# Who makes the low part of a weight tile: VectorE by a subtraction, or ScalarE and an accumulating DMA

## The chip, the cores and the metric

The kernel runs on one NeuronCore of a Trainium2 chip. The metric is the device time of one execution in microseconds, from launch to end; lower is better. Engines are called as in the profile: PE is TensorE's matrix multiplications, PEld its weight loads, DVE is VectorE, ACT is ScalarE, POOL is GpSimd, SP is SyncE. SP and POOL start most of the transfers here; the transfers themselves run on 16 DMA engines.

## The reference, cut to what matters

Two layers of a transformer work on 128 prompt tokens and 512 sample tokens of width 1024. Each layer has three token mixers side by side (a retention, a differential attention and a latent attention, called MLA), merged through sigmoid gates, and then a gated feed-forward net (FFN) of inner width 2816. All is float32. What matters is that nearly everything is a product of activations and weights:

```python
def _layer(x, mod, lw, lam_init, rope, ctx):
    sh1, sc1, g1, sh2, sc2, g2 = jnp.split(mod, 6, axis=-1)
    h = _rmsnorm(x, lw['norm1_g']) * (1.0 + sc1) + sh1
    mix, ctx_out = _mixers(h, lw, lam_init, rope, ctx)
    x = x + g1 * mix
    h = _rmsnorm(x, lw['norm2_g']) * (1.0 + sc2) + sh2
    x = x + g2 * _swiglu(h, lw['w_ffn_in'], lw['w_ffn_out'])
    return x, ctx_out

def _swiglu(h, w_in, w_out):
    a, b = jnp.split(h @ w_in, 2, axis=-1)
    return (jax.nn.silu(a) * b) @ w_out
```

## The kernel before, in words

A product in float32 is made of three products in a shorter format, float32r. Each operand is split into a high part, which is the value rounded to float32r, and a low part, which is what the rounding left out; then hi·hi + hi·lo + lo·hi is summed in one PSUM bank. Where the weights are the stationary operand, these are lines 131 to 133 (`mm3`) and 1087 to 1089 (`mm_outer`, which walks the contraction in the outer loop and several outputs in the inner one).

All weights pass through `load_w`, in 298 units. A unit is a tile of 128 rows and at most 1024 columns of float32, up to 512 KB: `raw` comes from DRAM by a transfer that SP starts (L120), ACT copies it into `whi` (L112, called from L123), and DVE subtracts `whi` from `raw` into `wlo` (L115, called from L124). The three kinds of tile rotate through buffers of their own: 3 for `raw`, 4 for `whi`, 4 for `wlo`. A buffer is used again when its last reader is done. So the copy of unit n waits until PE has gone through unit n - 4, and the transfer of unit n until the subtraction of unit n - 3 is done.

The work of a layer runs in this order. The latent attention (`mla`) has small weight units of its own (`w_qp`, `w_qk`, `w_v`), and between its steps `fill()` puts pieces of the differential attention's projections (`diff_proj`, six pairs of units), whose results go to DRAM by transfers that POOL starts (L773). Then come the first branch product, the differential attention with gates and retention values between its steps (stores by POOL, L790), the retention with the second merge, and the third merge (`branch`). `out_proj` and `ffn` follow. The FFN goes through 22 inner columns in three parts of 8, 8 and 6: for each column two `w_ffn_in` units (L1089 is the line that reads their low parts), and after each part eight `w_ffn_out` units (L1146). The FFN's opening makes its first two columns in halves, so that it needs four units at once and then the next two.

From the third merge of layer 0 on, `ada_rows` loads 80 blocks of modulation weights (`rawr`, 512 KB each, 3 buffers) by transfers that POOL starts (L235), and DVE reduces each in two instructions (L238).

The order of the instructions on each engine isn't the order of the program text: the framework plans it with a simulated timeline of its own and then writes one fixed list for each engine. Engines run their lists in order and wait on semaphores.

Of the kernel before, what the change touches and what calls it, by code (L numbers as in the profile page):

```python
# [12 lines left out]
F32 = mybir.dt.float32  # L13
# [8 lines left out]
P = 128  # L22
# [3 lines left out]
T = 640  # L26
# [9 lines left out]
NA = 416            # columns of the first product of the latent attention; 256 more follow  # L36
FFN_PARTS = ((0, 8), (8, 16), (16, 22))

# columns of the constant table
C_ID, C_ONE, C_DF, C_DB, C_SEL, C_VEC = 0, 128, 256, 384, 512, 514  # L40
C_C64, C_S64, C_C32, C_S32, C_END = 520, 776, 1032, 1160, 1288
# columns of the per-partition parameter table
V_ADA, V_N1, V_N2, V_FG, V_QN, V_KVN, V_END = 0, 96, 112, 128, 136, 142, 146
# columns of the replicated-row table
# [3 lines left out]
class Kern:  # L48
# [25 lines left out]
    def G(self):  # L74
        """A bank for a product: two in turn, one of them only while attention has the other."""
        self.gi ^= 1
        tag = "G" if self.gi or self.filling else "O"
        return self.ps.tile([P, 512], F32, tag=tag, name="G", bufs=1)
# [11 lines left out]
    def plan(self, points, *gens):  # L90
        """Spread the pieces of (generator, number of pieces[, from, to]) evenly over the next calls of fill()."""
        order = []
        for j, (_, n, *span) in enumerate(gens):
            t0, t1 = span or (0.0, 1.0)
            order += [(t0 + (t1 - t0) * (i + 0.5) / n, j) for i in range(n)]
        self.queue = [(t * points, gens[j][0]) for t, j in sorted(order)]
        self.point = 0
# [19 lines left out]
    def load_w(self, src, cols):  # L117
        """A weight unit [128, cols] from DRAM, as a part that float32r holds and the rest."""
        raw = self.w.tile([P, cols], F32, tag="raw", name="raw", bufs=3)
        self.nc.sync.dma_start(out=raw, in_=src)  # L120
        hi = self.w.tile([P, cols], F32R, tag="whi", name="whi")
        lo = self.w.tile([P, cols], F32R, tag="wlo", name="wlo")
        self.split_hi(hi, raw)  # L123
        self.split_lo(lo, raw, hi)  # L124
        return hi, lo

    def mm3(self, out, steps):
        """out = sum of lhsT^T rhs over steps of (lhs_hi, lhs_lo, rhs_hi, rhs_lo)."""
        n = len(steps)
        for i, (lh, ll, rh, rl) in enumerate(steps):  # L130
            self.pe.matmul(out, lh, rh, start=i == 0, stop=False)  # L131
            self.pe.matmul(out, lh, rl, start=False, stop=False)  # L132
            self.pe.matmul(out, ll, rh, start=False, stop=i == n - 1)  # L133

    def rsqrt(self, out, ssq, n, mul, mul2=1.0):
        """out = mul2 / sqrt(ssq * mul + EPS), for [128, n]."""
        v = self.sm.tile([P, n], F32, tag="rs_v", name="rs_v")
        a = self.sm.tile([P, n], F32, tag="rs_a", name="rs_a")
        y = self.sm.tile([P, n], F32, tag="rs_y", name="rs_y")
        self.dve.tensor_scalar(v, ssq, mul, EPS, op0=ALU.mult, op1=ALU.add)  # L140
        self.dve.tensor_scalar(y.bitcast(I32), v.bitcast(I32), 1, None, op0=ALU.arith_shift_right)
        self.dve.tensor_scalar(y.bitcast(I32), y.bitcast(I32), -1, 0x5F3759DF, op0=ALU.mult, op1=ALU.add)
        for it in range(4):
            self.dve.tensor_tensor(a, y, y, op=ALU.mult)
            self.dve.scalar_tensor_tensor(a, a, -0.5, v, op0=ALU.mult, op1=ALU.mult)
            self.dve.scalar_tensor_tensor(out if it == 3 else y, a, 1.5, y, op0=ALU.add, op1=ALU.mult)
        if mul2 != 1.0:
            self.dve.tensor_scalar(out, out, mul2, None, op0=ALU.mult)
# [7 lines left out]
    def setup(self):  # L156
# [12 lines left out]
        # silu of the two conditioning vectors, padded to 32 columns  # L169
# [7 lines left out]
    def rows_setup(self):  # L177
        # log_sigmoid(x) = min(x, 0) - log1p(exp(-|x|)), log1p(e) = 2 atanh(e / (2 + e))
# [38 lines left out]
    def ada_vectors(self, pool):  # L217
        """silu of the two conditioning vectors on every partition."""
        d = self.dve
        cs = self.csr = self.load_small(pool, [P, 2, 1024], self.io["condr"], "csr")  # L220
        for i in range(2):
            th = pool.tile([P, 1024], F32, tag="rawr", name="csth", bufs=3)
            self.act.activation(th, cs[:, i, :], AF.Tanh, scale=0.5)
            d.scalar_tensor_tensor(th, th, 1.0, cs[:, i, :], op0=ALU.add, op1=ALU.mult)
            d.tensor_scalar(cs[:, i, :], th, 0.5, None, op0=ALU.mult)

    def ada_rows(self, l, b0, b1, pool):
        """Modulation with output columns on partitions and the sums on VectorE, a column block a step."""
# [16 lines left out]
    def mod_scale(self, l, which):  # L245
        """A = norm_g * (1 + sc) as [128, 8, 2]; which 0 for the mixers, 1 for the ffn."""
# [10 lines left out]
    def square(self, h, k, x, pool):  # L257
        """Adds the squares of row tile k of a half of x to its sum."""
# [26 lines left out]
    def modulate(self, l, which, h, k, xn, a, ht, pool):  # L285
        """Row tile k of h = xn * A + sh, in float32r parts."""
# [13 lines left out]
    def norm(self, l, which, h, x, a, pool, ps):  # L300
        """h-th half of rmsnorm(x) * A + sh from the sum of squares, in float32r parts (hi, lo) [128, 8, n]."""
# [9 lines left out]
    def start(self):  # L311
        """First norm and first part of the first product, as the columns of the modulation come in."""
# [79 lines left out]
    def tok(self, act, k, b):  # L392
        """(hi, lo) stationary block b of an activation in two halves."""
# [4 lines left out]
    def a_steps(self, act, b, units):  # L398
        """For 128 tokens of block b, act^T W; units: list of (hi, lo, first k, n k) with [128, nk, N]."""
# [17 lines left out]
    def rope(self, pool, out, x, b, nb, nh, hd, tag="avs"):  # L417
        """out = rope(x) for sample blocks b .. b + nb: x [128, nb, nh, hd]."""
# [13 lines left out]
    def softmax(self, sv, p, z, scale, tot=None):  # L432
        """p = exp(scale (sv - max sv)), tot = sum p, z = 1 / tot, for one score row a partition in sv."""
# [7 lines left out]
    def mla(self, l, act, yraw, pool, first=None):  # L441
# [10 lines left out]
        # the k tiles hold two heads each time: rows 0:64 k_nope, rows 64:96 k_pe  # L452
        NK = 3
        kts = [pool.tile([P, 2, TK], F32R, name=f"kt{i}") for i in range(NK)]
        for g in range(2):
# [12 lines left out]
            if g == 0:  # L468
                self.rsqrt(rs[:, 0, :], ss[:, 0, :], NB, 1.0 / 256)
                # decoupled keys  # L470
# [15 lines left out]
                # compressed keys and values  # L486
# [43 lines left out]
        # decoupled queries of all heads, by tokens  # L530
# [81 lines left out]
    def mla_av(self, pool, v, hh, blks, pt, n, y, last=None):  # L612
        """y [64, n] += p^T v over key blocks; pt(kb) gives (hi, lo) [128, n]."""
# [11 lines left out]
    def mla_head(self, pool, qt, q0, kt, v, hh, y, last=None):  # L625
        """Two blocks of sample queries of one head."""
# [55 lines left out]
    def diff(self, l, act, yhi, ylo, ctx):  # L682
# [4 lines left out]
        # lambda  # L687
# [12 lines left out]
        def build(hd):  # L700
# [8 lines left out]
            # keys  # L709
# [24 lines left out]
            # queries, as hi(q1) lo(q1) lo(q2) hi(q2)  # L734
# [24 lines left out]
    def diff_proj(self, l, act, pool):  # L759
        """Queries, keys, values of the differential attention, by tokens, to DRAM; a generator."""  # L760
# [15 lines left out]
    def ret_values(self, l, act, pool):  # L776
        """Values and doubled silu gates of the retention, by tokens, to DRAM; a generator."""
# [15 lines left out]
    def diff_head(self, pool, Q, K1, K2, V, nlam, lam_init, yhi, ylo):  # L793
# [3 lines left out]
        for b in (1, 2, 3, 4, 0):  # L797
# [19 lines left out]
            # p0 / t0 - lam p1 / t1 = (p0 - (lam t0 / t1) p1) / t0, the last division after the product with v  # L817
# [39 lines left out]
    def ret(self, l, act, yraw, ctx):  # L857
# [6 lines left out]
        # decay matrices by (key, query), with the key scale  # L864
# [13 lines left out]
        # projections  # L878
        qkT = pool.tile([P, 2, 2, T], F32, name="qkT")       # (q, k), head pair: rows are 2 heads x 64
        QX = pool.tile([P, 4, T - 128], F32, name="QX")      # per head: rows xi_f q | xi_b q  # L880
        V = pool.tile([P, NB, 512], F32, name="rV")
        SG = pool.tile([P, NB, 512], F32, name="rSG")
        S0 = pool.tile([P, 4, 4, 128], F32, name="rS")       # block, head: states before the block (f | b)
# [5 lines left out]
        for which in (1, 0):  # L889
            units = self.load_a(io["w_ret"][l, which], 2, 4, 256)  # L890
            for b in range(NB):
# [23 lines left out]
                # sums over the chunk: forward states at once, backward ones once all are there  # L915
# [15 lines left out]
        for b in range(NB):  # L931
            self.fill()
            sc = self.S()                        # even heads in one bank, odd ones in the other
# [40 lines left out]
    def branch_first(self, l, g, yhi, ylo, m):  # L974
        """m = y W of the first branch; its gates come later."""
# [10 lines left out]
    def gates(self, l, g, act, m, pool):  # L986
        """m *= 2 sigmoid(gate logits); a generator."""
# [11 lines left out]
    def branch(self, l, g, act, yhi, ylo, m, pool, last):  # L999
        """m += 2 sigmoid(gate logits) * (y W); a generator."""  # L1000
# [50 lines left out]
    def tail(self, unit, load, n0, a, b, mid):  # L1051
        """Units (n, half) for n0 <= n < 8, half a's first; mid once half a is done."""
# [28 lines left out]
    def mm_outer(self, outs, steps, hook=None):  # L1081
        """Products of which each one's row tile k comes before row tile k + 1 of any; hook after a few."""
# [10 lines left out]
    def ffn(self, l, act, x, pool, xp, hook, a, b, mid):  # L1093
# [21 lines left out]
        # the first two columns by halves, the second half's norm within the first half's products  # L1115
# [159 lines left out]
def consts():  # L1275
# [5 lines left out]
    dist = i[None, :] - i[:, None]                # query minus key, at (key, query)  # L1281
# [23 lines left out]
def ntiles(w):  # L1305
    """[K, N] -> [N / 128, 128, K / 128 * 128]: column tiles, rows on partitions."""
# [4 lines left out]
def pieces(w, nk):  # L1311
    """[K, N] -> [K / 128 / nk, 128, nk N]."""
# [4 lines left out]
def layout(inputs):  # L1317
# [17 lines left out]
    st = np.concatenate([g["state_ret_fwd"][0], g["state_ret_bwd"][0]], axis=2)     # l, h, 128, 128  # L1335
# [59 lines left out]
```

## Time and profile before

| | |
|---|---|
| time, median of 2 runs | 2521.03 us (2520.76 to 2521.29) |
| the profiled execution's own time, first to last instruction | 2522.9 us |
| PE busy | 2471.6 us (98%) |
| DVE busy | 1500.7 us (59%) |
| ACT busy | 987.9 us (39%) |
| POOL busy | 170.8 us (7%) |
| mean granted TensorE clock | 0.995 |
| SP's queue of weight transfers | 164.12 MB, 19.6% of 16 engines' span |
| POOL's queue of transfers | 81.36 MB, 9.8% |

The profile is of one execution on the chip. Its span, from the first to the last instruction, is 2522.9 us, which is 1.9 us over the median of the timed runs; there is no other measure of that execution, so sums made against the profile are made against this span. "Busy" counts an engine's own instructions. A wait is put down to the instruction whose semaphore came last. The chain is followed back from the last instruction through what released each step.

### The profile page before, as it was taken

To read this page: it belongs to the slowest core of one execution; us is meant where nothing else is said; L and a number is where in the kernel's file an instruction comes from. 1 tells how busy PE (TensorE), PEld (TensorE's weight loads), DVE (VectorE), ACT (ScalarE), POOL (GpSimd) and SP (SyncE) were. 2 spreads that over 40 slices of the span, in tenths; PEclk is the share of its full clock that TensorE was granted. 3 is DMA by queue.
4 is the path that set the end of the run, shared out by engine and by line. 5 is a ranking of instruction groups with operands and counts; after the bars stand their busy time and mean duration, and the time that the engine had idled before them with its cause. 6 is when DMAs were issued, how large, how long until landed. Compare 5 with 4: busy or idle time off the path is not lost.

```text
span 2522.9 us, 42747 instructions
## 1 busy us (share of the span) xinstructions
PE 2471.6 (98%) x17236; PEld 2378.8 (94%) x17236; DVE 1500.7 (59%) x3439; ACT 987.9 (39%) x2102; POOL 170.8 (7%) x298
## 2 busy tenths in 40 slices
PE   8999999999999999999999999999999999999997
PEld 5999988899999999999999998889999999999997
DVE  5877665466798676585477866655663562323334
ACT  5656454532324322222376654554222352122123
POOL 0000210010010000010000012001000000000001
PEclk9999999999999999999999999999999999999999
DMA  6212321131553454453231123113222221222221
GB/s 259 76 56 70 101 65 52 64 132 59 186 182 126 142 164 157 139 184 107 65 126 60 52 76 115 62 44 114 79 96 88 72 71 67 84 68 84 67 74 61
DMA packets 70677, 248.94 MB, mean 99 GB/s; under 512 B 9840, under 2 KB 10064, under 8 KB 69584
## 3 DMA queue, kind: packets, MB, share of 16 engines
q1 hardware_dynamic: 46944, 164.12, 19.6%
q0 software_dynamic: 23248, 81.36, 9.8%
q8 instruction: 135, 2.21, 0.4%
q10 hardware_dynamic: 288, 0.73, 0.1%
q14 instruction: 62, 0.51, 0.1%
HBM read 225.97 MB, written 20.22 MB: 98 GB/s over the span
## 4 chain that ended last, share of the span: by engine, by line
PE 91%; issue 3%; DVE 3%; ACT 2%; DMA 1%; POOL 0%; DVEq 0%; ACTq 0%; POOLq 0%
PE G L131 13%; PE G L132 12%; PE G L133 12%; PE S L1089 8%; PE S L1088 8%; PE S L1087 8%; PE S L131 6%; PE S L132 6%; PE S L133 6%; PE S L808 2%; PE S L807 1%; PE Tp L645 1%; PE O L837 1%; PE O L620 1%; PE O L619 1%
## 5 line engine op out<-in xcount | busy, mean ns | idle before, releaser
L112 ACT CAST whi<-raw 128x1024 fp32r<-128x1024 f32 (+4 forms) x298 | 299.2, 1018 | 755.6 <-PE G L132 265.4
L115 DVE TENSOR_TENSOR wlo<-raw,whi 128x1024 fp32r<-128x1024 f32 (+4 forms) x298 | 349.1, 1182 | 358.4 <-ACT whi L112 356.2
L131 PE MATMUL G<-ghi,whi 128*128 128x256 f32 (+1 forms) x704 | 217.2, 309 | 3.1 <-DVE x L1049 3.1
L133 PE MATMUL G<-ghi,wlo 128*128 128x384 f32 (+1 forms) x704 | 216.5, 308 | 0.0
L132 PE MATMUL G<-glo,whi 128*128 128x384 f32 (+1 forms) x704 | 216.4, 308 | 0.0
L1087 PE MATMUL S<-h1hi,whi 128*128 128x384 f32 x640 | 214.0, 334 | 0.0
L1088 PE MATMUL S<-h1lo,whi 128*128 128x384 f32 x640 | 213.9, 334 | 0.0
L1089 PE MATMUL S<-h1hi,wlo 128*128 128x384 f32 x640 | 213.9, 334 | 0.0
L1089 PE MATMUL S<-h0hi,wlo 128*128 128x256 f32 x704 | 199.2, 283 | 1.0 <-DVE wlo L115 0.9
L1088 PE MATMUL S<-h0lo,whi 128*128 128x256 f32 x704 | 198.8, 283 | 0.0
L1087 PE MATMUL S<-h0hi,whi 128*128 128x256 f32 x704 | 198.1, 283 | 0.0
L238 DVE SCALAR_TENSOR_TENSOR junk<-rawr,csr 128x1024 bf16<-128x1024 f32 x160 | 194.9, 1218 | 1.3
L131 PE MATMUL G<-whi,h1hi 128*128 128x256 f32 x624 | 179.3, 288 | 2.7 <-ACT rvs L786 1.0
L133 PE MATMUL G<-whi,h1lo 128*128 128x256 f32 x624 | 177.9, 285 | 0.0
L132 PE MATMUL G<-wlo,h1hi 128*128 128x256 f32 x624 | 177.1, 284 | 0.0
L1049 DVE SCALAR_TENSOR_TENSOR x<-G,mod,x 128x128 f32<-128x128 f32 (+1 forms) x192 | 77.4, 435 | 138.1 <-PE G L133 137.6
L435 DVE TENSOR_REDUCE mx<-S 128x1 f32<-128x640 f32 (+1 forms) x160 | 113.8, 714 | 75.1 <-PE S L808 53.6
L1089 PEld LDWEIGHTS S<-h0hi,wlo 128*128 128x128 f32 x704 | 134.6, 191 | 2.8 <-DVE wlo L115 2.5
L131 PEld LDWEIGHTS G<-ghi,whi 128*128 128x128 f32 x704 | 132.1, 188 | 4.6 <-DVE x L1049 3.3
L1088 PEld LDWEIGHTS S<-h0lo,whi 128*128 128x128 f32 x704 | 134.3, 191 | 0.3
L1087 PEld LDWEIGHTS S<-h0hi,whi 128*128 128x128 f32 x704 | 134.3, 191 | 0.0
L132 PEld LDWEIGHTS G<-glo,whi 128*128 128x128 f32 x704 | 132.1, 188 | 0.2
(428 smaller groups left out, 6908.0 us busy)
## 6 DMA issues: line engine op xcount, KB each, us to landing
raw<-w_ffn_in SPq DMA_DIRECT2D x88, 512.0 KB, 3.6
rawr<-w_adat POOLq DMA_DIRECT2D x80, 512.0 KB, 3.9
raw<-w_gate SPq DMA_DIRECT2D x48, 512.0 KB, 3.3
raw<-w_ffn_out SPq DMA_DIRECT2D x32, 512.0 KB, 3.7
raw<-w_diff SPq DMA_DIRECT2D x24, 512.0 KB, 3.4
raw<-w_branch SPq DMA_DIRECT2D x24, 512.0 KB, 3.7
raw<-w_ret SPq DMA_DIRECT2D x24, 512.0 KB, 3.3
raw<-w_ada SPq DMA_DIRECT2D x16, 512.0 KB, 9.7
```

Of the source, the lines that this page charges most:

```text
L112: (eng or self.act).copy(hi, src)
L115: (eng or self.dve).tensor_tensor(lo, src, hi.bitcast(F32), op=ALU.subtract)
L131: self.pe.matmul(out, lh, rh, start=i == 0, stop=False)
L132: self.pe.matmul(out, lh, rl, start=False, stop=False)
L133: self.pe.matmul(out, ll, rh, start=False, stop=i == n - 1)
L238: self.tc.keep_in_program_order(d.scalar_tensor_tensor(junk, raw, 1.0, self.csr[:, i, :], op0=ALU.mult, op1=ALU.mult, accum_out=mod[:, n, ...
L435: self.dve.tensor_reduce(mx, sv, axis=AX.XY if len(sv.shape) == 3 else AX.X, op=ALU.max)
L808: pe.matmul(o, Q[rows, c, q0:q0 + 128], K2[rows, k0:k0 + n], start=False, stop=True)
L1049: self.dve.scalar_tensor_tensor(x[h][:, n, c0:c1], ps[:, c0:c1], g[:, n, gi:gi + 1], x[h][:, n, c0:c1], op0=ALU.mult, op1=ALU.add)
L1087: self.pe.matmul(o, lh, rh, start=k == 0, stop=False)
L1088: self.pe.matmul(o, lh, rl, start=False, stop=False)
L1089: self.pe.matmul(o, ll, rh, start=False, stop=k == nk - 1)
```

## The change

`load_w` still copies `raw` into `whi` on ACT. Then ACT writes the negated value into `wlo`, which is of type float32r, so that it holds minus the high part; and POOL starts a transfer inside SBUF that reads `raw` and adds it to `wlo` in place. The DVE subtraction for weight tiles is gone; the other callers of `split_lo` keep it. Elsewhere the diff removes comments only.

```diff
     def load_w(self, src, cols):
         raw = self.w.tile([P, cols], F32, tag="raw", name="raw", bufs=3)
         self.nc.sync.dma_start(out=raw, in_=src)
         hi = self.w.tile([P, cols], F32R, tag="whi", name="whi")
         lo = self.w.tile([P, cols], F32R, tag="wlo", name="wlo")
         self.split_hi(hi, raw)
-        self.split_lo(lo, raw, hi)
+
+        self.act.activation(lo, raw, AF.Copy, scale=-1.0)
+        self.nc.gpsimd.dma_start(out=lo.bitcast(F32), in_=raw, accum_op=ALU.add)
         return hi, lo
```

## Rows read from the trace of the kernel before

**Rows 1.** The page's first line and part 1, busy time of each engine.

```profile
span 2522.9 us, 42747 instructions
PE 2471.6 (98%) x17236; PEld 2378.8 (94%) x17236; DVE 1500.7 (59%) x3439; ACT 987.9 (39%) x2102; POOL 170.8 (7%) x298
```

**Rows 2.** The page's part 4, the chain that ended last, by engine.

```profile
PE 91%; issue 3%; DVE 3%; ACT 2%; DMA 1%; POOL 0%; DVEq 0%; ACTq 0%; POOLq 0%
```

**Rows 3.** Waits of PE and PEld: us in total, times, longest us.

```profile
PEld S L1089 <- DVE wlo L115: 2.5, 5, 0.8
...
PE S L1089 <- DVE wlo L115: 0.9, 2, 0.4
```

**Rows 4.** The page's part 5, two groups: busy us, mean ns | idle before, what ended most.

```profile
L112 ACT CAST whi<-raw 128x1024 fp32r<-128x1024 f32 (+4 forms) x298 | 299.2, 1018 | 755.6 <-PE G L132 265.4
L115 DVE TENSOR_TENSOR wlo<-raw,whi 128x1024 fp32r<-128x1024 f32 (+4 forms) x298 | 349.1, 1182 | 358.4 <-ACT whi L112 356.2
```

**Rows 5.** Line 115's instructions on `wlo`: ns min/median/max, first and last start, forms.

```profile
L115 DVE TENSOR_TENSOR wlo<-raw,whi x298: 680/1224/1228, 22.6 to 2487.8; 128x1024 fp32r<-128x1024 f32 x130, 128x768 fp32r<-128x768 f32 x9, 128x832 fp32r<-128x832 f32 x4, 128x640 fp32r<-128x640 f32 x4
```

**Rows 6.** Timeline, FFN opening of layer 0: start us, us, instruction, [idle before].

```profile
831.07 1.05 ACT L112 CAST whi<-raw 128x1024 fp32r<-128x1024 f32 x1 [7.22 <-PE G L1088]
...
832.16 1.23 DVE L115 TENSOR_TENSOR wlo<-raw,whi 128x1024 fp32r<-128x1024 f32 x1 [7.66 <-ACT whi L112]
...
833.44 0.19 PEld L1089 LDWEIGHTS S<-h0hi,wlo 128*128 128x128 f32 x1 [0.40 <-DVE wlo L115]
```

**Rows 7.** Timeline, a `w_qk` unit of the latent attention of layer 0.

```profile
77.80 0.82 DVE L115 TENSOR_TENSOR wlo<-raw,whi 128x640 fp32r<-128x640 f32 x1
...
80.36 0.19 PEld L133 LDWEIGHTS S<-ckh,wlo 128*128 128x128 f32 x1
```

**Rows 8.** Timeline, a pair of `w_ffn_in` units in the FFN's steady part, layer 0.

```profile
861.32 2.00 ACT L112 CAST whi<-raw 128x1024 fp32r<-128x1024 f32 x2 [5.49 <-PE S L1088]
...
862.41 2.36 DVE L115 TENSOR_TENSOR wlo<-raw,whi 128x1024 fp32r<-128x1024 f32 x2 [5.53 <-ACT whi L112]
...
876.36 0.19 PEld L1089 LDWEIGHTS S<-h0hi,wlo 128*128 128x128 f32 x1
```

**Rows 9.** Timeline, the first `w_ffn_out` unit of a part, layer 0.

```profile
904.63 1.22 DVE L115 TENSOR_TENSOR wlo<-raw,whi 128x1024 fp32r<-128x1024 f32 x1 [5.53 <-ACT whi L112]
...
909.91 0.19 PEld L133 LDWEIGHTS G<-ghi,wlo 128*128 128x128 f32 x1
```

**Rows 10.** Line 223's instructions: an ACT activation of 128x1024, ns min/median/max.

```profile
L223 ACT ACTIVATE csth<-csr x2: 1046/1049/1052, 652.6 to 653.6; 128x1024 f32<-128x1024 f32 x2
```

**Rows 11.** DMA issues: queue, count, KB each, median us from issue to landing.

```profile
raw<-w_ffn_in SPq DMA_DIRECT2D x88, 512.0 KB, 3.6
rawr<-w_adat POOLq DMA_DIRECT2D x80, 512.0 KB, 3.9
...
dproj<-stg POOLq DMA_DIRECT2D x60, 128.0 KB, 2.0
...
x<-x POOLq DMA_DIRECT2D x1, 1024.0 KB, 7.9
xs<-x POOLq DMA_DIRECT2D x1, 1024.0 KB, 4.1
x<-xs POOLq DMA_DIRECT2D x1, 1024.0 KB, 5.3
```

**Rows 12.** The page's part 3: packets, MB, share of 16 engines.

```profile
q1 hardware_dynamic: 46944, 164.12, 19.6%
```

**Rows 13.** POOL's groups of instructions from 800 to 1270 us, columns as in rows 4.

```profile
L235 POOL DMA_DIRECT2D rawr<-w_adat x53 | 28.0, 529 | 332.4 <-DVE junk L238 327.6 <-issue 4.8
```

**Rows 14.** POOL's waits from 800 to 1270 us, columns as in rows 3.

```profile
POOL rawr L235 <- DVE junk L238: 327.6, 51, 43.3
```

**Rows 15.** Busy us by stretch: latent attention and FFN of layer 0; PEclk, DMA share, GB/s.

```profile
64.00:280.00 216.00, 211.92 (x1663) 206.40 (x1661) 163.38 (x409) 132.18 (x320) 21.64 (x40) 1.00 0.21 69
800.00:1270.00 470.00, 466.77 (x3174) 464.42 (x3173) 295.30 (x515) 129.84 (x210) 28.56 (x54) 1.00 0.42 135
```

## The prediction, made before the changed kernel was run

> **What bounds the kernel now.** I read the page's head and its chain first. PE is busy 2471.6 of 2522.9 us [rows 1] and holds 91% of the chain, against 3% for DVE and 2% for ACT [rows 2]. So the 349 us that DVE spends on weights are nearly all beside PE's work, and taking them off DVE buys little: all idle time of PE together is 2522.9 - 2471.6 = 51.3 us, and that includes the start and the end of the program, which no weight tile touches. That is an upper bound on any gain, just 2.0%.
>
> The question then is the reverse: does a low part that comes later make PE wait? Today it hardly ever does. The waits name a `wlo` only where the FFN reads it, 2.5 us on PEld and 0.9 us on PE [rows 3]. Next I took from the timeline, for each of the 298 units [rows 5], its margin: the first PEld on its `wlo` minus the end of its subtraction. Four kinds are shown. In the FFN's opening the subtraction starts at 832.16, ends at 833.39 and PEld follows at 833.44: margin 0.05 us [rows 6]. A small unit of the latent attention: 77.80 + 0.82 to 80.36, 1.7 us [rows 7]. The first `w_ffn_out` unit of a part: 904.63 + 1.22 to 909.91, 4.1 us [rows 9]. The FFN's steady part, second unit of a pair: 862.41 + 2.36 to 876.36, 11.6 us [rows 8]. Over all units 6 margins are under 1 us, 19 under 3, 39 under 5.2 and 131 under 12. The margins are this short because of the four buffers: ACT's copy waits for PE to free one (755.6 us of idle time stand before these copies, and PE ended most of it) [rows 4], so preparing a unit cannot simply start earlier.
>
> **The change part by part.** Removed: 298 DVE subtractions, 1.22 us for a full one [rows 5], 349 us in all [rows 4]. Most hide behind PE, so I cost the removal at nothing on the path, except that DVE's own part of the preparation goes.
>
> Added on ACT: 298 activations. The nearest row is an activation of the same shape, 1049 ns [rows 10], like a full copy's 1.05 us [rows 6]. So they cost what the copies cost, 299 us [rows 4]: ACT goes from 988 to some 1290 of 2523 us, 51%. In the latent attention ACT goes from 132 to about 151 of 216 us (19 units) [rows 15]. Behind the activation on ACT stands the next unit's copy, in the FFN pairs back to back [rows 8], so the second unit of a pair comes 1.05 us later still. On the chain I set ACT's increase against DVE's decrease: 2% of the span times 300/988 is +15 us, 3% times 349/1501 is -18 us. I take zero for both.
>
> Added on POOL: 298 issues, about 0.53 us each by the issue of an equally large transfer [rows 13], 158 us; POOL is at 7%. Each waits for ACT, and behind it in POOL's list stand the `rawr` loads and the stores of the attention projections; that is a rival below. On SP nothing is issued anew, but a `raw` buffer now comes free only when the addition has landed, so the transfer three units later starts later, with 3.6 us to land [rows 11]. In the steady part that fits into the 11.6 us.
>
> Added on the DMA engines, and this decides: the landing of the addition. No row has an accumulating transfer. It moves 512 KB, but has to read two tiles and write one. Lower bound: a plain copy out of SBUF, 2.0 us for 128 KB and 4.1 for 1024 KB, by a straight line 2.9 us for 512 KB. Upper bound: a transfer of 1024 KB at its slowest, 7.9 us. Between them stands 1024 KB from DRAM into SBUF, 5.3 us [rows 11]. I take 5.3, since an addition is nearest to a transfer of twice the bytes into SBUF, on the same queue. Engine time: 164.12 MB hold 19.6% of the span, 494 us, so one 512 KB unit holds the engines for 1.6 us [rows 12]; I take 3.0 for an addition, and let the additions queue at that. All of them hold 298 x 3.0 = 0.9 ms of engine time, on engines that are 42% busy at most in a long stage [rows 15].
>
> The Trainium skill's page "Collectives: The Full Stack" (The bandwidth ceiling: the fold count and why AG ≠ RS ≠ AR) says that an add inside the DMA costs what its second source read costs and nothing for the arithmetic. "DMA: Bandwidth & Descriptors" (Anatomy of one DMA, SWDGE path) prices a transfer at 2.0 us plus bytes / 436e3; for 1 MiB that is an estimate of 4.4 us, where the rows have 4.1 to 7.9, and with it the sum below would be 47 us in place of 70.
>
> The sum. Before, `wlo` is there 0.04 + 1.23 us after the copy [rows 6]. After, 1.05 + 0.1 (semaphores, an estimate, twice the 0.04 us between copy and subtraction there, rounded up) + 5.3 = 6.45 us after it. So each low part is 5.2 us late, and 39 of 298 margins are shorter. Taken singly, their shortfalls add to 91 us. But a stall also delays what follows, so I replayed all units in order: the copy of n moves with the freeing of n - 4, `raw` with the landing of n - 3, ACT and the additions queue, and PE stalls by what is missing. The total is 70 us: 35 in the latent attentions (11 units, 16 us in layer 0 and 19 in layer 1), 21 in the two FFN openings (8 units, 11 and 10 us), 5 at the first `w_ffn_out` units and neighbours, 7 in the merges, 2 at the start and in the output projection. The steady FFN loses nothing. 70 on 2522.9 is 2.8%; the profiled span is 1.9 us above the median, so on the median the same sum gives 2521 + 70 = 2591 us.
>
> With 2.9 us the same replay gives 17 to 21 us, with 4.1 some 40, with 6.5 107, with 7.9 157 us. A measurement of this kernel can tell about 2%, 50 us, from no change; the replay passes that at 4.5 us.
>
> **The rivals.** (1) Not slower: the addition is cheap. If it lands in 4.5 us or less, the margins take most of it, and the loss is 17 to 50 us, 2538 to 2571. For it: copies out of SBUF land in 2.0 and 4.1 us. The planner works the same way: in the latent attention it can put a piece of `diff_proj` where a unit is late, which takes up to 35 us off the sum. Against: the copy into SBUF on POOL's queue, `rawr`, takes 3.9 us for one reading alone [rows 11]. The point from which it decides is 4.5 us.
>
> The figure of 4.4 us from "DMA: Bandwidth & Descriptors" in the Trainium skill would put the kernel here, at 2568.
>
> (2) POOL's list blocks. From 800 to 1270 us POOL stands at the head of its list waiting for DVE to free a `rawr` buffer, 51 times, 327.6 us in all, 6.4 us in the mean [rows 14]. An addition that is planned behind such a load waits as well. If each of the 87 units from 640 to 1262 us is 6.4 us later, the replay gives 175 us in place of 70: 2696. For it: `rawr` waits fill 70% of that stretch. Against: the list is planned in simulated time, and there these loads come late; DVE also gets faster.
>
> (3) The addition is slow, because the transfer is cut into small pieces or works at a fraction of a copy's rate. At 7.9 us, 157 us; from some 9 us on the steady FFN's 11.6 us are used up, and at 10 us, with 6 us of engine time for each, the replay gives 350 us, 2870. Nothing in the profile speaks for it but that no such transfer is there.
>
> (4) Faster: the planner makes use of an emptier DVE. It would have to win nearly all of PE's 51.3 us of idle time to show.
>
> **How the numbers follow.** Landing between 4.5 and 6.5 us, 50 to 107 us lost: 0.38, the forecast, at 2591. Rival 1: 0.34. Rival 2, with landings up to 7.9 us: 0.20, 2628 to 2700. Rival 3: 0.06. Rival 4: 0.02. The range goes from the lowest price, 2538, to rival 2's end, 2700; above it lies rival 3, below it rival 4 and a planner that hides everything. Slower by over 2% (over 2571) is the forecast, rivals 2 and 3: 0.64. Within 2%: 0.34. Faster: 0.02. The likeliest case alone spans 2571 to 2628.
>
> **What would show it.** Right: DVE near 1152 us busy and ACT near 1290; some 300 additions on POOL's queue with 512 KB and 5 to 6 us to landing; PE and PEld waits on a DMA into `wlo`, 60 to 90 us, a half of them in the latent attentions and a third at the FFN openings (near 805 to 835 us and 2045 to 2075 us, shifted); none in the steady FFN. Wrong: a landing under 4.5 us with PE idle as before (rival 1); additions that POOL issues several us after ACT is done, with `rawr` ahead of them (rival 2); waits on `wlo` at every FFN column (rival 3); or PE's order changed so much that these units no longer stand where they did.

## The result, and the profile after

The changed kernel takes 2597.73 us (median of 2 runs, 2594.91 to 2600.55) against 2521.03 us: a ratio of 1.030, 95% interval 1.028 to 1.032, slower by 76.7 us. The profiled execution lasts 2598.8 us, 75.9 us more than the one before. The page's head and its part 1:

```profile
span 2598.8 us, 43285 instructions
PE 2493.7 (96%) x17236; PEld 2396.6 (92%) x17236; DVE 1183.6 (46%) x3141; ACT 1251.6 (48%) x2400; POOL 428.9 (17%) x596
```

Beside [rows 1]: DVE lost 317 us of work and the time rose; PE executes the same 17236 instructions. Its busy time rose by 22.1 us and its idle time from 51.3 to 105.1 us, by 53.8: together the 75.9. The new instructions are in part 5 (negation, addition), to be read against the subtraction of [rows 4]:

```profile
L126 POOL DMA_DIRECT2D wlo<-raw x298 | 254.9, 855 | 1513.4 <-ACT wlo L125 1372.2
L125 ACT ACTIVATE wlo<-raw 128x1024 fp32r<-128x1024 f32 (+4 forms) x298 | 304.6, 1022 | 47.4 <-PE G L134 34.6
```

The DMA issues after, with the median landing as the last column, and the two big queues of part 3 (before: [rows 11, 12]):

```profile
wlo<-raw POOLq DMA_DIRECT2D x260, 512.0 KB, 5.4
raw<-w_ffn_in SPq DMA_DIRECT2D x88, 512.0 KB, 4.6
rawr<-w_adat POOLq DMA_DIRECT2D x80, 512.0 KB, 6.3
...
rproj<-rvs POOLq DMA_DIRECT2D x40, 128.0 KB, 3.0
```

```profile
q0 software_dynamic: 66160, 231.85, 40.6%
q1 hardware_dynamic: 46944, 164.12, 19.0%
```

An addition lands in 5.4 us. Its neighbours became slower: 3.6 to 4.6 us for `w_ffn_in`, 3.9 to 6.3 us for `rawr`. Now the waits, first PE's (line, what it waited for: us in total, times, longest), then PEld's on `wlo`, then POOL's:

```profile
PE S L1091 <- DMA wlo<-raw: 19.5, 7, 5.0
PE G L133 <- DVE rvs L791: 11.8, 9, 3.2
...
PE S L135 <- DMA wlo<-raw: 6.5, 7, 2.3
...
PE G L133 <- ACT rvs L788: 5.7, 8, 1.2
PE S L1090 <- DMA wlo<-raw: 4.4, 1, 4.4
```

```profile
PEld S L1091 <- DMA wlo<-raw: 22.1, 8, 5.3
PEld S L135 <- DMA wlo<-raw: 8.1, 7, 2.5
PEld S L1090 <- DMA wlo<-raw: 4.7, 1, 4.7
```

```profile
POOL wlo L126 <- ACT wlo L125: 1372.2, 249, 31.4
POOL rawr L237 <- DVE junk L240: 158.4, 67, 6.7
```

The reader should see three things. PE now waits for a landing in `wlo` where it hardly waited before [rows 3]: 30.4 us in the three lines. It also waits for `rvs`, the eviction of the retention's value products, which is not a weight tile; the same wait in the trace of before was small:

```profile
PE G L131 <- DVE rvs L789: 1.7, 5, 0.4
...
PE G L131 <- ACT rvs L786: 1.0, 2, 0.5
```

And POOL nearly always waits for ACT's negation; its wait for `rawr` buffers, 327.6 us between 800 and 1270 us alone before [rows 14], is down to 158.4 us in the whole run.

By stage: the differential attention, the FFN's opening with the first part of eight columns, and the rest of the FFN, all of layer 0; first before, then after (from:to and length in us; busy us of PE, PEld, DVE, ACT, POOL; granted clock; DMA share; GB/s).

```profile
282.00:543.20 261.20, 257.31 (x1760) 231.80 (x1761) 154.73 (x432) 124.89 (x325) 34.83 (x57) 0.99 0.25 83
803.60:909.80 106.20, 105.68 (x724) 104.57 (x724) 69.11 (x127) 40.73 (x71) 5.28 (x10) 1.00 0.40 126
909.80:1273.60 363.80, 361.10 (x2452) 359.85 (x2451) 226.19 (x390) 88.72 (x137) 23.28 (x44) 1.00 0.43 138
```

```profile
292.50:563.80 271.30, 260.58 (x1761) 235.37 (x1762) 131.40 (x411) 145.21 (x347) 54.81 (x80) 0.97 0.47 124
828.40:948.60 120.20, 110.74 (x723) 109.23 (x723) 47.20 (x96) 54.56 (x86) 17.18 (x23) 0.94 0.66 167
948.60:1310.30 361.70, 360.24 (x2453) 359.37 (x2452) 176.51 (x347) 133.57 (x188) 70.55 (x99) 1.00 0.81 215
```

The opening got 14 us longer, the differential attention 10 us; the long FFN stretch, with the most additions and the DMA engines 81% busy, got 2 us shorter. The second column of numbers to watch is the granted clock: 0.94 in the opening, where it was 1.00. Three windows show how that looks close up, around a wait of 3.14 us for `wlo` that ends at 839.0:

```profile
835.60:839.00 3.40, 0.26 (x4) 0.06 (x2) 2.52 (x6) 3.39 (x7) 0.00 (x0) 1.00 0.73 165
...
839.60:843.00 3.40, 3.40 (x19) 3.40 (x18) 1.92 (x4) 1.35 (x3) 0.00 (x0) 0.50 0.53 154
843.00:846.40 3.40, 3.40 (x28) 3.40 (x28) 0.06 (x1) 0.47 (x2) 0.00 (x0) 1.00 0.00 0
```

```profile
838.99 0.39 PE L1091 MATMUL S<-h0hi,wlo 128*128 128x256 f32 x1 [3.14 <-DMA wlo<-raw]
...
840.21 0.41 PE L1089 MATMUL S<-h0hi,whi 128*128 128x256 f32 x1
840.42 0.41 PE L1090 MATMUL S<-h0lo,whi 128*128 128x256 f32 x1
...
843.46 0.28 PE L1091 MATMUL S<-h0hi,wlo 128*128 128x256 f32 x1
843.57 0.28 PE L1089 MATMUL S<-h0hi,whi 128*128 128x256 f32 x1
```

PE stood nearly still in the first window, and right behind it runs at a granted clock of 0.50, which is the level of 1.2 GHz: 19 instructions where the next 3.40 us, at 2.4 GHz, hold 28. The timeline has products of the same shape start 0.21 us apart there and 0.12 us apart behind it. So this wait costs 3.14 us of idle time and, with 16 products at the slower pace, some 1.5 us more that count as busy. Over the whole run the mean granted clock fell from 0.995 to 0.985: by the clock, (1 - 0.985) x 2598.8 = 39 us lost against (1 - 0.995) x 2522.9 = 13 us before. That difference, 26 us, is about the 22.1 us by which PE's busy time grew.

### The profile page after: what moved, and what is told of

The parts are those of the page before. It is cut to its first block, busy times and chain, and to the rows that moved or that the text cites. A ratio compares the mean times of both kernels' runs of the same rounds, so it can differ in the third digit from the quotient of the medians.

```text
span 2598.8 us, 43285 instructions
## 1 busy us (share of the span) xinstructions
PE 2493.7 (96%) x17236; PEld 2396.6 (92%) x17236; DVE 1183.6 (46%) x3141; ACT 1251.6 (48%) x2400; POOL 428.9 (17%) x596
## 3 DMA queue, kind: packets, MB, share of 16 engines
q0 software_dynamic: 66160, 231.85, 40.6%
## 4 chain that ended last, share of the span: by engine, by line
PE 56%; issue 29%; DMA 7%; POOL 4%; ACT 2%; DVE 1%; POOLq 0%; SPq 0%; DVEq 0%; ACTq 0%
PE G L133 7%; PE G L134 7%; PE G L135 7%; PE S L1091 4%; PE S L1090 4%; PE S L133 4%; PE S L1089 4%; PE S L135 4%; PE S L134 4%; DMA wlo<-raw 3%; POOL wlo L126 3%; PE S L810 1%; DMA rawr<-w_adat 1%; POOL rawr L237 1%; DMA raw<-w_ada 1%
## 5 line engine op out<-in xcount | busy, mean ns | idle before, releaser
L126 POOL DMA_DIRECT2D wlo<-raw x298 | 254.9, 855 | 1513.4 <-ACT wlo L125 1372.2
L125 ACT ACTIVATE wlo<-raw 128x1024 fp32r<-128x1024 f32 (+4 forms) x298 | 304.6, 1022 | 47.4 <-PE G L134 34.6
L1091 PE MATMUL S<-h0hi,wlo 128*128 128x256 f32 x704 | 204.0, 290 | 19.6 <-DMA wlo<-raw 19.5
L133 PE MATMUL G<-ghi,whi 128*128 128x384 f32 (+1 forms) x704 | 216.1, 309 | 1.7 <-DVE x L1051 1.6
L1108 DVE TENSOR_TENSOR fs<-fs,S 128x256 f32<-128x256 f32 x84 | 40.6, 484 | 360.6 <-ACT fs L1107 360.4
L1091 PEld LDWEIGHTS S<-h0hi,wlo 128*128 128x128 f32 x704 | 138.5, 197 | 22.4 <-DMA wlo<-raw 22.1
```

The costliest lines, as they stand in the source:

```text
L125: self.act.activation(lo, raw, AF.Copy, scale=-1.0)
L126: self.nc.gpsimd.dma_start(out=lo.bitcast(F32), in_=raw, accum_op=ALU.add)
L1091: self.pe.matmul(o, ll, rh, start=False, stop=k == nk - 1)
```

## The experiments

Each run has the kernel before beside it on the same chip; a gain or loss is the difference of the two medians. A stage begins with PE's first instruction of its kind in the timeline. "Ready" is the median, over the units, of the time from the start of a unit's high-part copy until its low part is complete; it is 2.31 us before and 7.29 us after.

**The negation without the transfer.** ACT negates as in the change, and DVE adds.

```diff
-        self.nc.gpsimd.dma_start(out=lo.bitcast(F32), in_=raw, accum_op=ALU.add)
+        self.dve.tensor_tensor(lo, raw, lo.bitcast(F32), op=ALU.add)
```

> ScalarE still writes the negated high part, but VectorE adds the raw tile in place of the DMA, so low parts are early again (about 1 us later than before the change) and ScalarE keeps its extra 305 us. Theory L (late low parts alone cost the 76 us, with the half-clock stretches behind the waits): both FFN openings back to 106 to 111 us each, both differential-attention stages back to 261 to 264 us, total 2523 to 2535 us. Theory A (the differential-attention stages lose their 10 us each to ScalarE's longer list, not to the DMA): openings back, but those stages stay at 269 to 273 us; total 2543 to 2562 us.

2564.97 us, ratio 1.018 (1.016 to 1.020), 45 us lost with no added transfer and the low part ready at 3.27 us; that is 3 us above the second theory's range. The openings are nearly as before (218.6 us for both layers against 216.3), the differential attentions 22 us longer and the latent ones 20 us. So these two stages can lose their time without a late landing, and taking the landing away gives back only 32 of the 77 us.

**The transfer without ACT's negation.** DVE negates.

```diff
-        self.act.activation(lo, raw, AF.Copy, scale=-1.0)
+        self.dve.tensor_scalar(lo, raw, -1.0, None, op0=ALU.mult)
```

> VectorE writes the negated tile in place of ScalarE; the DMA still adds. ScalarE is back to its load before the change, low parts stay about 5 us late. Theory L: nothing of weight changes, openings 118 to 122 us, differential-attention stages 269 to 273 us, total 2585 to 2602 us. Theory A: openings 118 to 122 us, but the differential-attention stages back to 261 to 264 us, total 2562 to 2582 us.

2579.45 us, 1.023 (1.022 to 1.025). ACT is back at 990 us busy, yet the differential attentions still lose 18 us. That ACT is the busier engine is therefore not their cause. The total lies where the second theory had it and the stages where the first did. The openings lose 37 us here, but the rest of the FFN is 12 us shorter than before: the FFN as a whole loses 25 us, as with the change (24).

**A short addition.** Only the first 128 columns are added; the others keep minus the high part.

```diff
-        self.nc.gpsimd.dma_start(out=lo.bitcast(F32), in_=raw, accum_op=ALU.add)
+        self.nc.gpsimd.dma_start(out=lo.bitcast(F32)[:, 0:128], in_=raw[:, 0:128], accum_op=ALU.add)
```

> The DMA adds only the first 128 columns of each unit; the rest of the low part is left as the negated high part, so an eighth to a quarter of the bytes move and the issue, the waits and ScalarE's load stay. Landing about 2.5 us in place of 5.4. Theory L: openings 107 to 114 us, all else within a few us of before, total 2528 to 2542 us. Theory A: openings 107 to 114 us, differential-attention stages still 269 to 273 us, total 2548 to 2565 us. Should the fixed part of the transfer be what is late, landing over 4 us and openings at 118 to 122 us.

2562.09 us, 1.016 (1.015 to 1.018). The landing:

```profile
wlo<-raw POOLq DMA_DIRECT2D x298, 64.0 KB, 2.4
```

3.0 us less to land gives back 35 of the 77 us; 42 stay. The landing is a large term. How much of the 42 us is something else this run can't say: the low part is ready at 4.74 us, still 2.4 us later than before.

**The opening's units by subtraction.** `load_w` gets a flag `sub` for the old way; here it is set for the first three columns of `w_ffn_in`, 12 of 298 units.

```diff
+        if sub:
+            self.split_lo(lo, raw, hi)
+        else:
             self.act.activation(lo, raw, AF.Copy, scale=-1.0)
             self.nc.gpsimd.dma_start(out=lo.bitcast(F32), in_=raw, accum_op=ALU.add)
...
-                wu[f, j] = self.load_w(io["w_ffn_in"][l, f, j], 1024)
+                wu[f, j] = self.load_w(io["w_ffn_in"][l, f, j], 1024, f < 3)
```

> The first six w_ffn_in units of each layer get their low part by the old VectorE subtraction, all other 286 units by the DMA. Both theories: openings back to 106 to 111 us each and the half-clock stretches near 840, 867, 2113 and 2140 us gone, differential-attention stages unchanged at 269 to 273 us; total 2570 to 2580 us. Rival: the loss there is only moved, to the next short margins or to the steady FFN, total 2588 us or more.

2577.52 us, 1.022 (1.020 to 1.024). The two openings, from first product to the first `w_ffn_out` product:

```profile
830.90:937.80 106.90, 105.92 (x723) 104.59 (x722) 51.05 (x104) 51.43 (x83) 14.73 (x20) 1.00 0.62 163
2089.40:2199.50 110.10, 109.58 (x747) 108.67 (x746) 35.07 (x74) 54.17 (x87) 10.13 (x12) 1.00 0.50 125
```

They take 217 us, as before, at a granted clock of 1.00: 4% of the units carry the openings' whole loss, waits and lost clock alike. DMA engines that are 62% busy in one of them do it no harm.

**The retention's units by subtraction.** The flag is set for `w_ret`, 24 units.

```diff
-            units = self.load_a(self.io["w_ret"][l, 2 + j], 2, 4, 256)
+            units = self.load_a(self.io["w_ret"][l, 2 + j], 2, 4, 256, True)
...
-            units = self.load_a(io["w_ret"][l, which], 2, 4, 256)
+            units = self.load_a(io["w_ret"][l, which], 2, 4, 256, True)
```

> The units of w_ret keep the VectorE subtraction; all others are prepared by the negation and the accumulating DMA. Theory of late readiness (the w_ret products that cover the end of a differential-attention stage come too late when their low part takes 5 us more): both differential-attention stages go back to 261 to 265 us (271 and 272 with the change), and the total to 2575 to 2582. Rival, a fragile plan (any change of costs lets the planner order TensorE's work worse there): these stages stay at 266 to 275 us and the total at 2585 to 2600. The FFN openings stay at about 120 us by both.

2586.19 us, 1.026 (1.024 to 1.027): 12 us of 77 come back. The differential attentions take 264.6 and 267.2 us (after: 271.2 and 272.1): one within what the theory expected, one within what its rival expected, and the total is where the rival expected it. Of that stage's 20.3 us, 11.5 come back with these 24 units; the rest stays, so their preparation is a part of its loss and not all of it. Their lateness and their negation are given back together here and not told apart.

**All units with short margins by subtraction.** The flag is set for `w_ret`, the first three `w_ffn_in` columns, and all units of the latent and differential attention's products, 86 in all.

```diff
-        wh, wl = self.load_w(io["w_qp"][l], 768)
+        wh, wl = self.load_w(io["w_qp"][l], 768, True)
...
-            wh, wl = self.load_w(io["w_v"][l, j], 512)
+            wh, wl = self.load_w(io["w_v"][l, j], 512, True)
...
-            wh, wl = wu[pr] = self.load_w(io["w_qk"][l, pr], 640)
+            wh, wl = wu[pr] = self.load_w(io["w_qk"][l, pr], 640, True)
...
-                units = self.load_a(self.io["w_diff"][l, hp, kind], 2, 4, 256)
+                units = self.load_a(self.io["w_diff"][l, hp, kind], 2, 4, 256, True)
...
```

> VectorE subtraction for every unit outside the streams of w_gate, w_branch, w_out, the FFN's weights from the fourth w_ffn_in on and w_ffn_out; only those streams use the accumulating DMA. If the loss is late readiness where the margin is short, the total is at most 2535 (before 2520), the differential-attention stages 261 to 265 and the FFN openings 106 to 111. If accumulations beside the streams cost in themselves, or the plan is fragile, it is 2545 or more.

2547.61 us, 1.010 (1.009 to 1.012). 51 of 77 us come back, and 26 stay, more than the theory allowed and where its rival had the total. The profiled execution, which lost 20, has 11 of them in merges and output projections and 6 in the differential attentions, where gate units are prepared.

**Only the FFN's streams by the transfer.** `w_gate`, `w_branch` and `w_out` go back too; the addition is left for 124 units, `w_ffn_in` from the fourth column on and `w_ffn_out`. (The expectation's "about 150" was a miscount.)

```diff
-            u = self.load_w(self.io["w_gate"][l, g, n], 1024)
+            u = self.load_w(self.io["w_gate"][l, g, n], 1024, True)
...
```

> As the run with only the streams by the accumulating DMA, but w_gate, w_branch and w_out are also given back to the VectorE subtraction; the DMA adds only for the FFN's weights from the fourth w_ffn_in on and for w_ffn_out (about 150 units). If the 26 us that were left there came from late gate and branch units (differential attention and merges), the total is 2521 to 2530 and these stages are within 2 us of before. If accumulations cost PE something wherever they run, the FFN stages lose and the total is 2540 or more.

2523.55 us, 1.0007 (0.9998 to 1.0016): no difference. 124 additions, 42% of all, cost nothing that shows where the margins are long, and the rival, by which additions cost PE something wherever they run, falls. The engines' part 1 for this run:

```profile
PE 2466.6 (98%) x17236; PEld 2374.2 (94%) x17236; DVE 1366.9 (54%) x3315; ACT 1096.8 (43%) x2226; POOL 278.4 (11%) x422
```

DVE is 134 us lighter than before and nothing comes of it: that work was hidden.

**A plan upset by any change?** The kernel before, with each subtraction in two halves.

```diff
-        self.split_lo(lo, raw, hi)
+        c = cols // 2
+        self.split_lo(lo[:, :c], raw[:, :c], hi[:, :c])
+        self.split_lo(lo[:, c:], raw[:, c:], hi[:, c:])
```

> The kernel before, with each VectorE subtraction written as two of half the size: some 0.2 us more for each unit, no DMA and no work for ScalarE. Theory of late readiness: the total stays at 2519 to 2528 and the differential-attention stages at 261 to 263. Rival, a fragile plan (any added instruction reorders TensorE's work): these stages take 266 or more and the total is 2535 or more.

2526.35 us, 1.0015 (1.0005 to 1.0024), the differential attentions at 262.9 and 263.5 us. 298 more instructions on DVE do not upset the plan, so the rival falls in the form in which any change does. It does not fall in the form in which this change leads to a worse order of PE's products; that is taken up below.

**The negation first.** Negation and addition stand ahead of the copy in the program.

```diff
-        self.split_hi(hi, raw)
         self.act.activation(lo, raw, AF.Copy, scale=-1.0)
         self.nc.gpsimd.dma_start(out=lo.bitcast(F32), in_=raw, accum_op=ALU.add)
+        self.split_hi(hi, raw)
```

> The changed kernel with the negation and the accumulating DMA ahead of the copy that writes the high part, so the low part is ready about 1 us earlier and the high part 1 us later. If lateness of the low part by about 5 us sets the loss, the FFN openings get 1 to 2 us shorter each and the total is 2588 to 2597 (2597.7 with the change). If the high part was as late as the low one, or the plan decides, the total is 2597 to 2610.

2596.63 us, 1.030 (1.028 to 1.032), between the two ranges expected. It tells nothing: the framework put the copy first again at the opening (copy at 827.95, negation at 829.68 us), and the low part is ready at 7.24 us, as with the change.

**The addition in two halves.**

```diff
-        self.act.activation(lo, raw, AF.Copy, scale=-1.0)
-        self.nc.gpsimd.dma_start(out=lo.bitcast(F32), in_=raw, accum_op=ALU.add)
+        c = cols // 2
+        for a, b in ((0, c), (c, cols)):
+            self.act.activation(lo[:, a:b], raw[:, a:b], AF.Copy, scale=-1.0)
+            self.nc.gpsimd.dma_start(out=lo[:, a:b].bitcast(F32), in_=raw[:, a:b], accum_op=ALU.add)
```

> The changed kernel with the negation and the accumulating DMA each written as two halves of a unit, so that the first half's addition starts about 0.5 us earlier and moves half the bytes (3.5 us to land was seen for 256 KB, 5.4 for 512 KB). If the time until the addition has landed sets the loss, readers of the first half wait some 2 us less and the total is 2570 to 2590. If the second issue on POOL and two transfers at once eat this up, the total is 2595 to 2615.

2592.21 us, 1.028 (1.026 to 1.030), between the two expectations. A half landed in 4.4 us, not 3.5, and the last half is ready at 7.30 us, no earlier than the whole. The `rvs` waits grew, to 8.0 us for one:

```profile
PE G L135 <- DVE rvs L793: 19.1, 6, 8.0
PE S L1093 <- DMA wlo<-raw: 13.7, 7, 3.4
```

**ACT's work alone.** The kernel before, and ACT copies `raw` onto itself behind the subtraction: the change's work for ACT, no transfer, no later low part.

```diff
         self.split_lo(lo, raw, hi)
+        self.act.copy(raw, raw)
```

> The kernel before with one more ScalarE copy for each unit, of the raw tile onto itself once the subtraction has read it: ScalarE gets the 300 us of work that the change gives it, the low part is as early as before, no transfer is added. If ScalarE's longer list is itself what costs some 45 us in the runs with a negation, the total is 2545 or more and the latent and differential attentions lose. If only a later low part costs, the total is 2519 to 2532.

2531.85 us, 1.0043 (1.0028 to 1.0058): 12 us, at the upper end of what was expected if only lateness costs. ACT carries even more than with the change:

```profile
PE 2473.1 (98%) x17236; PEld 2378.3 (94%) x17236; DVE 1503.1 (59%) x3439; ACT 1267.7 (50%) x2400; POOL 170.5 (7%) x298
```

The low part is ready at 2.31 us, the differential attentions lose 0.7 us together, and the latent attentions 8.2. Here ACT's extra work stands behind the low part, and in the change ahead of it; that difference is not tested.

**Lateness alone.** The kernel before, and POOL moves each finished low part onto itself by a plain transfer.

```diff
         self.split_lo(lo, raw, hi)
+        self.nc.gpsimd.dma_start(out=lo.bitcast(F32), in_=lo.bitcast(F32))
```

> The kernel before with a plain transfer of each low part onto itself, started by GpSimd behind the subtraction: the low part is ready later by one landing, ScalarE and VectorE work as before. By the landings of plain copies inside SBUF it lands in 3 to 4.5 us. If the lateness of the low part is most of the loss, the total is 2555 to 2595 with the FFN openings at 115 us or more each; if ScalarE's work is half of it, it is 2535 to 2555. The landing also tells what the addition costs over a plain copy.

2587.24 us, 1.026 (1.024 to 1.028): 67.5 us, with the work of ACT and DVE as before; the openings take 248.4 us together, 32 more. This is what was expected if lateness is most of the loss. The landing, though, is longer than the 3 to 4.5 us expected. The transfer, POOL's queue, and PE's waits in this run:

```profile
wlo<-wlo POOLq DMA_DIRECT2D x260, 512.0 KB, 5.4
```

```profile
q0 software_dynamic: 63728, 231.85, 23.4%
```

```profile
PE S L1090 <- DMA wlo<-wlo: 19.4, 7, 5.6
...
PE G L133 <- DMA wlo<-wlo: 6.4, 5, 2.8
PE S L134 <- DMA wlo<-wlo: 5.9, 4, 3.1
PE G L132 <- DVE rvs L790: 5.2, 4, 2.4
```

The low part is ready at 8.18 us here, 5.9 us later than before, where the change makes it 5.0 us later; so 67.5 us is more than the change's own lateness would cost by itself. These 67.5 us and the 12 us of ACT's work make 80, beside 76.7 with the change, but that is no proof of a sum of two parts: the stages below do not add up, and the run with DVE adding loses 45 us with hardly any lateness. The mean granted clock is 0.987, nearly as low as with the change, so lateness alone can lose most of that clock.

Where each kernel lost, in us of the profiled span against the 2522.9 us of before, both layers taken together; the last column is the prediction's replay. (The profiled execution with DVE adding was 8 us slower than that run's median.)

| stage | the change | lateness alone | ACT's work alone | ACT negates, DVE adds | replay |
|---|---|---|---|---|---|
| start | +5.7 | +14.0 | -1.7 | -3.3 | 1 |
| latent attention | +17.1 | +10.1 | +8.2 | +19.9 | 35 |
| differential attention | +20.3 | +1.7 | +0.7 | +22.1 | 0 |
| merges, output projection | +8.7 | +6.3 | -2.8 | +2.9 | 8 |
| FFN openings and first part | +24.4 | +32.1 | +3.1 | +2.3 | 21 |
| rest of the FFN | -0.3 | -0.5 | -0.3 | +4.8 | 5 |

(The replay's 2 us for start and output projection are put half and half, and its 5 us at the first `w_ffn_out` units and neighbours to the last row.)

## Why the prediction was right, and where it was not

**The landing.** Taken at 5.3 us, measured at 5.4. "Each low part is 5.2 us late" was measured as 7.29 - 2.31 = 5.0 us. But the reason given, that an addition is nearest to a transfer of twice the bytes, does not hold: a plain transfer of 512 KB inside SBUF also lands in 5.4 us. The lower bound of 2.9 us, a straight line through copies out of SBUF on the same queue [rows 11], was too low for a copy that stays inside SBUF, so the right value came by luck, from a row that only happened to be as long. The addition shows in the engines' time instead: POOL's queue took 40.6% of 2598.8 us, less the 9.8% of 2522.9 us that it had before, is 808 us or 2.7 us for each addition (taken: 3.0); for the plain transfer (23.4% of 2586.6 - 247) / 298 = 1.2 us. Both take the queue's other transfers as they were before.

The Trainium skill's page "Collectives: The Full Stack" (The bandwidth ceiling: the fold count and why AG ≠ RS ≠ AR) prices an add by its second source read: the engine time agrees (2.7 us against 1.2), the landing does not show it. The formula of "DMA: Bandwidth & Descriptors" (Anatomy of one DMA, SWDGE path) gives an estimate of 3.2 us for the plain 512 KB and 4.4 us for double the bytes, where both landed in 5.4 us; the measurement decides.

**The sum.** 70 us predicted, 76.7 measured, 67.5 by a somewhat greater lateness alone. That lateness can cost this much is shown by that run; that it is the whole loss of the change is not, since a landing 3.0 us shorter gave back 35 us and no added transfer at all 32. By stages the near agreement is partly luck: 18 us too many in the latent attentions, 20 too few in the differential ones. Behind this stand two errors of the replay, one each way, and a stage that it did not have. First, "PE stalls by what is missing" left out the clock: of the change's 75.9 us, PE's idle time is 53.8 and its longer busy time 22.1, and the waits on `wlo` on PE are 30.4 us in the three lines shown, not "60 to 90" (PEld's are the same stretches). Of all of them, 32.7 us, 19.5 lie at the FFN openings and 8.9 in the latent attentions, where the prediction had a third and a half. The replay's unit of loss was too small, since behind a wait such as that of 839.0 us PE works at half its clock. Second, the replay kept PE's order. The framework planned a new one with the new costs: in the latent attention of the lateness run PE goes through its products in another order than before, waits 6.7 us on `wlo`, and the stage loses 10 us where the replay had 35. That other work was put where a unit was late is read from this, and not tested. Rival 1 had named this reordering.

**The FFN.** "21 in the two FFN openings" and "the steady FFN loses nothing" held: +24.4 us at the openings, -0.3 us in the rest, and 124 additions there without any effect. Giving 12 units back to DVE brought the openings back, so the margins of [rows 6] and [rows 8], 0.05 and 11.6 us, tell the two apart as the prediction said.

**ACT against DVE.** Set to zero on the chain. ACT's added work alone measured 12 us, so the +15 us of the prediction's own estimate was near; of DVE's -18 us nothing was seen in the run with the FFN's streams (134 us less DVE, no gain). The busy times came near what was predicted, DVE 1184 us (1152) and ACT 1252 us (1290). An issue on POOL was taken at 0.53 us and took 0.855.

**What the prediction did not have: the differential attention, 20 us.** There no low part of a weight makes PE wait. Neither more work nor a late low part suffices: ACT's work alone loses 0.7 us there, lateness alone 1.7, but every kernel in which a negation of the `w_ret` units stands on ACT or DVE loses more (22 with DVE adding, 18 with DVE negating, 11 with the short addition; 8.8 and 5.8 in the two runs that give `w_ret` back but not the gates). What PE loses there is accounted for: over both layers its waits for `rvs` grew from 2.7 to 17.5 us, and four more stretches of 3.41 us at half clock lose 6.8 us. And PE's order is another one. With lateness alone PE goes through the 1760 products of this stage in exactly the order of before, in both layers; in every kernel that loses over 5 us there, it does not. A new order is not enough for the loss, though: with all short margins by subtraction the order is new as well, and layer 0 takes 262.2 us, 1.0 more than before. How PE comes to wait for `rvs` stands in the timeline of the changed kernel, first ACT, then POOL, then PE:

```profile
517.67 1.06 ACT L125 ACTIVATE wlo<-raw 128x1024 fp32r<-128x1024 f32 x1 [0.60 <-PE G L134]
519.57 1.05 ACT L125 ACTIVATE wlo<-raw 128x1024 fp32r<-128x1024 f32 x1
520.52 0.36 ACT L790 ACTIVATE rvs<-G 128x256 f32<-128x256 f32 x1
...
537.62 0.66 ACT L790 ACTIVATE rvs<-G 128x256 f32<-128x256 f32 x2 [3.43 <-DMA rproj<-rvs]
```

```profile
529.33 0.87 POOL L889 DMA_DIRECT2D rV<-rproj  x1
530.20 1.12 POOL L792 DMA_DIRECT2D rproj<-rvs  x2
```

```profile
521.40 0.39 PE L133 MATMUL G<-whi,h0hi 128*128 128x256 f32 x1 [1.99 <-DVE rvs L791]
...
538.50 0.38 PE L133 MATMUL G<-whi,h1hi 128*128 128x256 f32 x1 [2.78 <-DVE rvs L791]
```

The eviction `rvs` of the first wait stands in ACT's list behind the preparation of two new units, and PE waits for its bank. At the second, the eviction waits for an `rvs` buffer whose store, issued behind a load of 640 KB, has not landed. The first is what the negation adds to an ordered list, as read from the timeline; the second also stands in the runs where `w_ret` was given back (3.0 and 5.3 us there), so the two were not separated. How much of the 20 us belongs to each, and what made the framework choose this order, stays open.

**The rivals.** (2) did not happen: all but 8 of the 298 additions start within 1 us of the end of their negation, and POOL waits for `rawr` only 158.4 us. (3) and (4) did not either. (1) was excluded by the landing of 5.4 us.

## What to carry to other kernels

Work that lay beside a full PE was worth nothing here when it was removed, and the delay of an operand cost where its margin was shorter: 124 units of 298 took 5 us more for nothing, and 12 units cost some 20 us. That is not the whole bill: new costs also gave PE a new order and put other instructions ahead of an eviction, and 20 us went in a stage where no weight was late. So measure the margin of each use, not the busy time of an engine, and give the slow path to the long streams alone; in this kernel even that only broke even, since DVE's time was free. Where a wait of some us is added to a PE that was hardly ever idle, expect a loss of clock right behind it, as behind the 3.14 us shown.

## What the runs showed of the hardware

A transfer of 512 KB from SBUF to SBUF on POOL's queue landed in 5.4 us (median) whether it added or only copied, an addition of 64 KB in 2.4 us; the addition held the DMA engines for 2.7 us each against 1.2, by the difference to the kernel before. Issuing an addition took POOL 855 ns in the mean, issuing the plain transfer of the same size 535 ns. Beside the additions the stores of 128 KB into `rproj` took 3.0 us in the median (2.0 before). And a wait of 3.14 us in an otherwise full stretch was followed by 3.40 us at a granted clock of 0.50.
